# Seven PSUM banks in place of five for one block of seven matmul groups

## The chip, the cores and the metric

The kernel runs on one core of a Trainium2 chip. Its metric is the time of one execution in device microseconds. Matmuls run on TensorE (PE in the profile), elementwise work on VectorE (DVE), ScalarE (ACT) and GpSimd (POOL); SyncE (SP) issues the transfers of weights. A core has eight PSUM banks of 128 x 512 fp32 values in this program, named b0 to b7.

## The reference

One layer of a hybrid decoder for 1024 prompt tokens and 64 sample tokens of width 1024, in fp32. The part that matters here is its MLP:

```python
h2 = rmsnorm(x, lw['g_mlp'])
x = x + jnp.square(jax.nn.relu(h2 @ lw['w_up'])) @ lw['w_down']     # w_up 1024 x 4096, w_down 4096 x 1024
```

Ahead of it stand the input projection, an RWKV-7 mixer, a short convolution and a stick-breaking attention; behind it a gate on a per-layer embedding.

## The kernel before

The tokens are split into two groups. Group A is 512 tokens, group B the other 576 (512 prompt tokens and the 64 of the sample), in two chunks of 288. The 4096 columns of the MLP are taken in 16 blocks of 256. For each block an `up` step computes 256 rows of relu squared (transposed: hidden rows on the partitions), and a `down` step multiplies them with 256 rows of `w_down` and adds the result to the residual `x`. Every fp32 operand is split into a high part in fp32r and a low part, the rest; a product is three matmuls (high by high, low by high, high by low), which are the lines L1094 to L1096 of the ordinary product (`gemm_p`) and L1453 to L1455 of the one below.

Group B's `up` step is `up7`. It computes its 2 x 2 blocks (two halves of the 256 columns by two halves of the 576 tokens) from seven products instead of eight, in the manner of Strassen and Winograd. `block_sums` (L1437 to L1440) forms four sums of weight blocks on DVE from two raw tiles `wr`; `split_piece` (L1074, L1075) casts each of the seven weight pieces to its high part `wh` or `wsh` on ACT and subtracts it for the low part `wl` or `wsl` on POOL or DVE. `seven` then issues the products in a fixed order of the source: (2,2), (3,3), (1,1), (11,11), (12,21), (4,22), (22,4), the first number being the weight piece and the second the operand, each 12 matmuls into one PSUM bank. ACT copies (11,11) out of PSUM as `p1` (L1461). DVE adds (L1509): `u2` = (2,2) + p1, `u3` = (3,3) + u2, `v` = (1,1) + u2, and the four results, each formed in the PSUM bank of the product that comes last for it. `out` (L1500 to L1502) takes a result from its bank with relu and the norm's factor (DVE), squares it (ACT), casts it to `ah` (ACT) and subtracts for `al` (POOL). `down` (L1522) has 16 products of 6 matmuls per block, each added to `x` by DVE.

The raw tiles `wr` have two buffers. A block uses them four times, two for `w_up` and two for `w_down`, each 512 KB, so that a transfer starts when DVE, ACT and POOL are done with what the buffer held before. Pieces `wh` and `wl` have ten buffers, `wsh` and `wsl` four.

Banks are handed out in turn by a function that `banks` returns:

```python
up_bank, down_bank = banks(0, 1, 2, 3, 4), banks(5, 6, 7)      # L1570
u = up7(B, 0, ops, hpb)
for fb in range(1, 16):
    u, before = up7(B, fb, ops, hpb), u
    down(*before, bank=down_bank)
```

The `up` step of block fb stands ahead of the `down` step of block fb - 1. The sixth product of a block so gets the bank of its first, the seventh that of its second, and the next block goes on from there. The order in which each engine has its instructions is not that of the source: a scheduler (L1748) sets it for the whole program ahead of the run, from its own estimates, so that a change of buffers in one place can move instructions from there to the end. On the chip each engine then takes them strictly in that order, and each waits for what it needs.

Group A's last products, ahead of `up7`, use the banks b0 to b5 in turn, and the norm of group B b6 and b7.

Of the kernel before, what the change touches and what calls it, by code (L numbers as in the profile page):

```python
# [48 lines left out]
def hybrid_step(ctx: ExitStack, tc: tile.TileContext, I, O):  # L49
# [6 lines left out]
    def f(t):  # L56
        return t.bitcast(F32)
# [9 lines left out]
    def banks(*ids):  # L67

        turn = itertools.cycle(ids)

        def take():
            i = next(turn)
            return psum.tile([128, 512], F32, name=f"b{i}", bufs=1)

        return take
# [782 lines left out]
    for hf in range(2):  # L858
        for n in range(3):
            w = W.load(w_in[:, SB0 + 512 * n + 256 * hf:SB0 + 512 * n + 256 * hf + 256])  # L860
# [210 lines left out]
    def split_piece(src, sub=None, pool=None, tag="w", bufs=10):  # L1071
        hl = [(pool or wpool).tile([128, 512], F32R, name=f"{tag}{e}", bufs=bufs) for e in "hl"]
        h3, l3 = (t.rearrange("p (k c) -> p k c", k=src.shape[1]) for t in hl)
        S.copy(h3, src)  # L1074
        (sub or G).tensor_sub(l3, src, f(h3))  # L1075
        return hl
# [354 lines left out]
    def block_sums(src, c0, s_, raw=(None, None)):  # L1431


        r = [raw_weights(src, 4 * k, 4, c0, 256, raw[k]) for k in range(2)]
        a = {(m, k): r[k][:, :, 128 * m:128 * m + 128] for m in range(2) for k in range(2)}
        s_ = [t.rearrange("p (k c) -> p k c", k=4) for t in s_]
        V.tensor_add(s_[0], a[1, 0], a[1, 1])  # L1437
        V.tensor_sub(s_[1], s_[0], a[0, 0])
        V.tensor_sub(s_[2], a[0, 0], a[1, 0])
        V.tensor_sub(s_[3], a[0, 1], s_[1])  # L1440
        return {2: s_[1], 3: s_[2], 1: s_[0], 11: a[0, 0], 12: a[0, 1], 4: s_[3], 22: a[1, 1]}

    def seven(w, ops, n, bank, held, add, out, behind=(), order=None):


        behind = iter(behind)

        def product(i, j):
            o = bank()[:, :n]
            wh, wl = (t.rearrange("p (k c) -> p k c", k=4) for t in w[i])  # L1450
            x = ops[j]
            for k in range(4):
                PE.matmul(o, wh[:, k], x[:, 0, k], start=k == 0, stop=False)  # L1453
                PE.matmul(o, wh[:, k], x[:, 1, k], start=False, stop=False)  # L1454
                PE.matmul(o, wl[:, k], x[:, 0, k], start=False, stop=k == 3)  # L1455
            next(behind, None)
            return o

        def first():
            p1 = held("p1")  # L1460
            S.copy(p1, product(11, 11))  # L1461
            return p1

        if order == "11 first":
            p1 = first()
            u2 = add("u2", product(2, 2), p1)
            u3 = add("u3", product(3, 3), u2)
            q5, q4 = product(1, 1), None
        else:
            q6, q7, q5 = product(2, 2), product(3, 3), product(1, 1)  # L1470
            q4 = product(22, 4) if order == "22 early" else None
            p1 = first()
            u2 = add("u2", q6, p1)
            u3 = add("u3", q7, u2)
        v = add("v", q5, u2)
        out(1, 1, add("c", q5, u3))
        if q4 is not None:
            out(1, 0, add("c", q4, u3))
        out(0, 0, add("c", product(12, 21), p1))
        out(0, 1, add("c", product(4, 22), v))  # L1480
        if q4 is None:
            out(1, 0, add("c", product(22, 4), u3))

    def up7(p, fb, ops, pool):


        s_ = [p.act("s", F32) for _ in range(2 * (fb == 0))]
        s_ = [s_[i // 2][:, i % 2, :512] if fb == 0 else pool.tile([128, 512], F32, name=f"s{i}") for i in range(4)]
        ws = {} if fb == 0 else dict(pool=pool, tag="ws", bufs=4)
        t = block_sums(w_up, fb * 256, s_)  # L1490
        w = {i: split_piece(t[i], **ws) if i < 11 else split_piece(t[i]) for i in t}
        n = p.n // 2
        ah, al = p.act("ah", F32R), p.act("al", F32R)
        ends = []

        def out(m, e, c):

            t = slice(e * n, e * n + n)
            r = p.tmp("c")[:, :n]
            V.scalar_tensor_tensor(r, c, 0.0, p.rb[:, t], op0=ALU.max, op1=ALU.mult)  # L1500
            S.square(r, r)
            ends[:] = [S.copy(ah[:, m, t], r), G.tensor_sub(al[:, m, t], r, f(ah[:, m, t]))]  # L1502

        def held(name):
            return pool.tile([128, n], F32, name=name)

        def add(name, c, t):
            r = c if name == "c" else held(name)
            V.tensor_add(r, c, t)  # L1509
            return r  # L1510

        seven(w, ops, n, up_bank, held, add, out)
        last_up[:] = ends
        return p, fb, ah, al

# [46 lines left out]
    ops = B.operands("g_mlp", (2, 3, 1, 4), mpb, 4)  # L1562
# [6 lines left out]
    hpb = tc.alloc_tile_pool(name="h_b", bufs=1, reuse_waits="tile")  # L1569
# [5 lines that stand above are left out]
# [124 lines left out]
    ops = {}  # L1699
    for m, end in enumerate(itertools.chain.from_iterable(gate(A, sl) for sl in range(4))):  # L1700
# [8 lines left out]
        if m == 6:  # L1709
            w = {}  # L1710
# [6 lines left out]
    for sl in range(4):  # L1717
        after = {}
        gate7(B, sl, ops, w, gate7_weights(sl + 1, after) if sl < 3 else ())
        w = after  # L1720
# [31 lines left out]
```

## Time and profile before

| | |
|---|---|
| median of 3 runs | 1705.01 us (1703.33 to 1708.07) |
| the profiled execution | 1706.69 us, of which the span from first to last instruction is 1705.1 |
| PE busy | 1637.8 us, 96% of the span |
| DVE, ACT, POOL busy | 65%, 48%, 43% |
| group B's MLP, from its first product to about its last | 1174.5 to about 1540 us |
| mean granted TensorE clock | 0.987 |

All times of the trace are in us from the start of the span. Matmuls are pipelined, so a row of the timeline shows 0.29 us for a matmul of 288 columns while the next one starts 0.13 us later; whether PE loses time is read from the starts, or from the idle time in brackets that a row shows ahead of it. In a timeline, "x2" is two instructions merged into one row, and a row of SP gives the time from the first issue to the end of the last. In the chain of waits a piece of a transfer gives the time from its issue to its landing.

### The profile page before, as it was taken

What the parts mean: (1) busy time and instruction counts of PE and PEld (TensorE: products, weight loads), DVE (VectorE), ACT (ScalarE), POOL (GpSimd) and SP (SyncE); (2) the same over time, 40 slices, a digit from 0 to 9 for tenths busy, and PEclk for the clock granted to TensorE, in tenths of its full rate; (3) what the DMA queues carried; (4) which work ended last, traced back from release to release, by engine and by line L of the source; (5) the groups of instructions that cost most, each with busy time, mean ns of one, the idle gap of its engine ahead of it and who ended that gap; (6) DMA issues with size and microseconds to landing.
All of it is one profiled execution on the core that took longest, in us unless ns stands there. A gap on an engine that the chain in (4) does not pass through costs nothing.

```text
span 1705.1 us, 30847 instructions
## 1 busy us (share of the span) xinstructions
PE 1637.8 (96%) x11853; PEld 1476.2 (87%) x11853; DVE 1105.0 (65%) x1918; ACT 820.7 (48%) x1627; POOL 727.3 (43%) x778
## 2 busy tenths in 40 slices
PE   6999899999899889999999999999999999999898
PEld 5899888889898767888887778987999999999698
DVE  6266844555277759888854345378777777764986
ACT  6633433343343657666543444364444334436753
POOL 4123121123232664443434654366655445538621
PEclk9999999999999999999999999999999999999999
DMA  5134466325523763433245665322322222323232
GB/s 189 49 120 124 142 166 178 72 78 158 160 66 96 226 170 124 137 121 116 78 121 149 187 178 189 112 84 77 97 90 87 87 87 90 98 76 105 87 120 56
DMA packets 212372, 202.26 MB, mean 119 GB/s; under 512 B 58305, under 2 KB 177761, under 8 KB 212098
## 3 DMA queue, kind: packets, MB, share of 16 engines
q1 hardware_dynamic: 202498, 179.33, 35.4%
q0 software_dynamic: 5120, 16.78, 3.3%
q10 hardware_dynamic: 4608, 4.20, 1.0%
q8 instruction: 93, 1.52, 0.4%
q14 instruction: 53, 0.43, 0.1%
HBM read 163.27 MB, written 36.98 MB: 117 GB/s over the span
## 4 chain that ended last, share of the span: by engine, by line
PE 76%; DVE 10%; DMA 6%; ACT 3%; issue 3%; SPq 2%; POOL 1%; ACTq 0%; DVEq 0%; POOLq 0%
PE b L1094 12%; PE b L1096 11%; PE b L1095 11%; PE b L1453 4%; PE b L1455 4%; PE b L1454 4%; PE b L169 3%; PE b L170 3%; PE b L171 3%; PE b L797 2%; PE b L795 2%; PE b L796 2%; PE b L942 2%; DMA wr<-in_w_in 1%; PE b L512 1%
## 5 line engine op out<-in xcount | busy, mean ns | idle before, releaser
L1075 POOL TENSOR_TENSOR wl<-wr,wh 128x512 fp32r<-128x512 f32 x182 | 255.1, 1411 | 265.5 <-ACT wh L1074 226.3
L1074 ACT CAST wh<-wr 128x512 fp32r<-128x512 f32 x308 | 187.9, 621 | 308.9 <-PE b L1095 198.0
L1522 DVE TENSOR_TENSOR x<-b,x 128x288 f32<-128x288 f32 (+1 forms) x384 | 199.2, 528 | 97.2 <-PE b L1096 86.0
L1094 PE MATMUL b<-ah,wh 128*128 128x288 f32 (+1 forms) x768 | 253.7, 331 | 3.2 <-DVE x L1522 2.1
L1096 PE MATMUL b<-ah,wl 128*128 128x288 f32 (+1 forms) x768 | 252.2, 328 | 0.0
L1095 PE MATMUL b<-al,wh 128*128 128x288 f32 (+1 forms) x768 | 252.0, 328 | 0.0
L1094 PEld LDWEIGHTS b<-ah,wh 128*128 128x128 f32 x768 | 144.5, 188 | 15.3 <-DVE x L1522 4.8
L1096 PEld LDWEIGHTS b<-ah,wl 128*128 128x128 f32 x768 | 144.5, 188 | 10.2
L1095 PEld LDWEIGHTS b<-al,wh 128*128 128x128 f32 x768 | 144.6, 188 | 9.3 <-DVE al L1426 0.3
L1094 PE MATMUL b<-nh,wh 128*128 128x512 f32 x320 | 129.1, 403 | 5.4 <-DVE x L1413 3.3
L795 PE MATMUL b<-wh,h_hi 128*128 128x256 f32 x432 | 127.4, 295 | 5.1 <-ACT sq L805 5.1
L1095 PE MATMUL b<-nl,wh 128*128 128x512 f32 x320 | 128.1, 400 | 0.0
L1096 PE MATMUL b<-nh,wl 128*128 128x512 f32 x320 | 127.7, 400 | 0.0
L797 PE MATMUL b<-wh,h_lo 128*128 128x256 f32 x432 | 126.8, 293 | 0.0
L796 PE MATMUL b<-wl,h_hi 128*128 128x256 f32 x432 | 124.7, 289 | 0.0
L1075 DVE TENSOR_TENSOR wl<-wr,wh 128x512 fp32r<-128x512 f32 x126 | 102.4, 815 | 26.4 <-ACT wh L1074 22.4
L159 POOL TENSOR_TENSOR wl<-wr,wh 128x1024 fp32r<-128x1024 f32 x26 | 64.6, 2500 | 123.0 <-ACT wh L158 118.0
L169 PE MATMUL b<-h_hi,wh 128*128 128x384 f32 (+1 forms) x336 | 115.1, 342 | 1.9 <-ACT xs L333 1.3
L170 PE MATMUL b<-h_lo,wh 128*128 128x384 f32 (+1 forms) x336 | 113.8, 339 | 0.3 <-DVE h_lo L201 0.3
L171 PE MATMUL b<-h_hi,wl 128*128 128x384 f32 (+1 forms) x336 | 112.5, 335 | 0.0
L922 DVE TENSOR_TENSOR_SCAN keep<-keep,onesq 128x128 f32<-128x128 f32 (+3 forms) x64 | 95.3, 1488 | 21.4 <-POOL keep L920 20.7
L1453 PE MATMUL b<-op,wh 128*128 128x288 f32 x320 | 95.0, 297 | 0.1
(437 smaller groups left out, 4450.6 us busy)
## 6 DMA issues: line engine op xcount, KB each, us to landing
wr<-in_w_up SPq DMA_DIRECT2D x64, 512.0 KB
wr<-in_w_down SPq DMA_DIRECT2D x64, 512.0 KB
wr<-in_w_in SPq DMA_DIRECT2D x26, 512.0 KB
wr<-in_w_out SPq DMA_DIRECT2D x16, 512.0 KB
wr<-in_w_ple_gate SPq DMA_DIRECT2D x16, 512.0 KB
xt<-in_x_prompt SPq DMA_DIRECT2D x8, 512.0 KB
stk_s<-sth ACTq DMA_DIRECT2D x32, 128.0 KB
stk_s<-stl SPq DMA_DIRECT2D x32, 128.0 KB
```

The source lines that it names most:

```text
L169: PE.matmul(ps[:, :n], wh[:, k, c], a, start=(k == 0), stop=False)
L170: PE.matmul(ps[:, :n], wh[:, k, c], b, start=False, stop=False)
L171: PE.matmul(ps[:, :n], wl[:, k, c], a, start=False, stop=(k == nk - 1))
L795: PE.matmul(o, a, w[0][:, k, :], start=(k == 0), stop=False)
L797: last = PE.matmul(o, b, w[0][:, k, :], start=False, stop=(k == 7))
L1074: S.copy(h3, src)
L1075: (sub or G).tensor_sub(l3, src, f(h3))
L1094: PE.matmul(ps[:, :n], w(0, k, m), a, start=(k == 0), stop=False)
L1095: PE.matmul(ps[:, :n], w(0, k, m), b, start=False, stop=False)
L1096: PE.matmul(ps[:, :n], w(1, k, m), a, start=False, stop=(k == nk - 1))
L1453: PE.matmul(o, wh[:, k], x[:, 0, k], start=k == 0, stop=False)
L1522: V.tensor_add(p.x[:, m, t0:t0 + n], ps[:, :n], p.x[:, m, t0:t0 + n])
```

## The change

For group B's first block the seven products get banks of their own, b0 to b6, handed out once; the five banks of `up_bank` are first taken up by the second block, which so starts at b0. Nothing else in the source differs (a blank line moves the lines behind by one: L1522 is L1523 there).

```diff
@@ -1509,7 +1509,8 @@
             V.tensor_add(r, c, t)
             return r

-        seven(w, ops, n, up_bank, held, add, out)
+
+        seven(w, ops, n, up_bank if fb else banks(*range(7)), held, add, out)
         last_up[:] = ends
         return p, fb, ah, al
```

The order of the engines' instructions is the same up to the fifth product of the first block and differs from there. Names below are a tile with its buffer number; b3_13057 is the fourth product, (11,11), of block 0, b4_13083 its fifth, b0_13102 or b5_13102 its sixth, b1_13121 or b6_13121 its seventh; 13182, 13195, 13208, 13222, 13248, 13267 and 13286 are block 1's products (2,2), (3,3), (1,1), (11,11), (12,21), (4,22) and (22,4); 13325 is block 0's first `down` product.

PE before, from the last matmul of block 0's fifth product; each row that is shown is the first of a product's 12:

```order
L1455 MATMUL b4_13083<-op21_12763,wl_13004 128x288
L1453 MATMUL b3_13195<-op3_12691,wsh_13156 128x288
...
L1453 MATMUL b0_13102<-op22_12764,wh_13007 128x288
...
L1453 MATMUL b1_13121<-op4_12693,wh_13011 128x288
...
L1453 MATMUL b2_13182<-op2_12690,wsh_13152 128x288
...
L1453 MATMUL b4_13208<-op1_12692,wsh_13160 128x288
...
L1453 MATMUL b0_13222<-op11_12762,wh_13164 128x288
...
L1453 MATMUL b1_13248<-op21_12763,wh_13168 128x288
...
L1094 MATMUL b5_13325<-ah_13015,wh_13307 128x288
```

PE with the change, over the same stretch:

```order
L1455 MATMUL b4_13083<-op21_12763,wl_13004 128x288
L1453 MATMUL b5_13102<-op22_12764,wh_13007 128x288
...
L1453 MATMUL b6_13121<-op4_12693,wh_13011 128x288
...
L1453 MATMUL b0_13182<-op2_12690,wsh_13152 128x288
...
L1453 MATMUL b1_13195<-op3_12691,wsh_13156 128x288
...
L1453 MATMUL b3_13222<-op11_12762,wh_13164 128x288
...
L1453 MATMUL b2_13208<-op1_12692,wsh_13160 128x288
...
L1453 MATMUL b4_13248<-op21_12763,wh_13168 128x288
...
L1094 MATMUL b5_13325<-ah_13015,wh_13307 128x288
```

Block 0's last two products now stand ahead of block 1's first; before, block 1's (3,3) stood ahead of them. Block 1's (11,11) is halved around (1,1).

DVE before, at block 1's additions; wl_13621 and wl_13625 are low parts of block 1's `w_down`, from the raw tile wr_13618:

```order
L1440 TENSOR_TENSOR s3_13456<-wr_13459,s1_13454 128x512
L1509 TENSOR_TENSOR u2_13236<-b2_13182,p1_13221 128x288
L1509 TENSOR_TENSOR u3_13238<-b3_13195,u2_13236 128x288
L1509 TENSOR_TENSOR v_13240<-b4_13208,u2_13236 128x288
L1075 TENSOR_TENSOR wl_13621<-wr_13618,wh_13620 128x512
L1509 TENSOR_TENSOR b1_13248<-b1_13248,p1_13221 128x288
L1509 TENSOR_TENSOR b4_13208<-b4_13208,u3_13238 128x288
L1075 TENSOR_TENSOR wl_13625<-wr_13618,wh_13624 128x512
```

DVE with the change:

```order
L1440 TENSOR_TENSOR s3_13456<-wr_13459,s1_13454 128x512
L1509 TENSOR_TENSOR u2_13236<-b0_13182,p1_13221 128x288
L1509 TENSOR_TENSOR b4_13248<-b4_13248,p1_13221 128x288
L1075 TENSOR_TENSOR wl_13621<-wr_13618,wh_13620 128x512
L1509 TENSOR_TENSOR u3_13238<-b1_13195,u2_13236 128x288
L1509 TENSOR_TENSOR v_13240<-b2_13208,u2_13236 128x288
L1075 TENSOR_TENSOR wl_13625<-wr_13618,wh_13624 128x512
L1509 TENSOR_TENSOR b2_13208<-b2_13208,u3_13238 128x288
```

The addition `u3` of block 1, which reads the bank of (3,3), stood ahead of wl_13621 and now stands behind it.

DVE with the change, from block 0's first additions to `x` on; s2_13768 is a weight sum of block 2 (L1439), wl_13631 a low part of block 1's second half of `w_down`:

```order
L1500 SCALAR_TENSOR_TENSOR c_13300<-b1_13286,rb_12589 128x288
L1439 TENSOR_TENSOR s2_13768<-wr_13770 128x512
L1075 TENSOR_TENSOR wl_13631<-wr_13628,wh_13630 128x512
L1523 TENSOR_TENSOR x_9357<-b6_13333,x_9357 128x288
L1523 TENSOR_TENSOR x_9357<-b5_13325,x_9357 128x288
L1523 TENSOR_TENSOR x_9357<-b7_13341,x_9357 128x288
L1523 TENSOR_TENSOR x_9357<-b5_13349,x_9357 128x288
```

Before, the additions of b6_13333 and b5_13325 stood ahead of s2_13768 and that of b7_13341 right behind it; now all three stand behind it and behind wl_13631.

## The prediction, on record before the run

> **What bounds the kernel now.** First the page: how much of the span TensorE works, and what the chain that ended last is made of.
>
> ```profile
> span 1705.1 us, 30847 instructions
> PE 1637.8 (96%) x11853; PEld 1476.2 (87%) x11853; DVE 1105.0 (65%) x1918; ACT 820.7 (48%) x1627; POOL 727.3 (43%) x778
> PE 76%; DVE 10%; DMA 6%; ACT 3%; issue 3%; SPq 2%; POOL 1%; ACTq 0%; DVEq 0%; POOLq 0%
> ```
>
> PE is the bound, so a change of banks can only give back time in which PE waits. The windows tell where that is: the first block's products up to the fifth, the stretch after them, the rest of the loop, and the gate at the end.
>
> ```profile
> core 0: us, PE busy (x) PEld busy (x) DVE busy (x) ACT busy (x) POOL busy (x), PEclk, DMA share, GB/s
> 1174.50:1182.50 8.00, 8.00 (x61) 7.91 (x59) 4.84 (x5) 2.84 (x6) 5.91 (x5) 1.00 0.30 92
> 1182.50:1210.00 27.50, 23.91 (x175) 23.05 (x174) 22.08 (x39) 15.00 (x33) 19.01 (x17) 1.00 0.35 108
> 1210.00:1540.00 330.00, 330.00 (x2492) 330.00 (x2491) 239.74 (x486) 135.01 (x280) 170.90 (x150) 1.00 0.30 91
> 1540.00:1705.00 165.00, 152.10 (x958) 139.28 (x956) 123.92 (x215) 91.76 (x183) 76.65 (x56) 0.97 0.30 88
> ```
>
> PE loses 27.50 - 23.91 = 3.6 us between 1182.5 and 1210, and nothing at all in the 330 us behind, at full clock. So this one stretch is what the change can touch directly. The waits of PE from 1165 to 1545 are three:
>
> ```profile
> PE b L1453 <- ACT p L1461: 1.5, 1, 1.5
> PE b L1453 <- DVE c L1500: 1.2, 1, 1.2
> PE b L1094 <- DVE x L1522: 0.7, 1, 0.7
> ```
>
> The timeline of PE gives their places (start, duration, and in brackets the idle time):
>
> ```profile
> 1182.37 0.29 PE L1455 MATMUL b<-op,wl 128*128 128x288 f32 x1
> 1184.18 0.40 PE L1453 MATMUL b<-op,wsh 128*128 128x288 f32 x1 [1.52 <-ACT p L1461]
> 1184.42 0.29 PE L1454 MATMUL b<-op,wsh 128*128 128x288 f32 x1
> 1186.17 0.40 PE L1453 MATMUL b<-op,wh 128*128 128x288 f32 x1
> 1190.82 0.40 PE L1453 MATMUL b<-op,wsh 128*128 128x288 f32 x1 [1.20 <-DVE c L1500]
> 1191.20 0.29 PE L1455 MATMUL b<-op,wsl 128*128 128x288 f32 x1
> 1197.19 0.29 PE L1455 MATMUL b<-op,wl 128*128 128x288 f32 x1
> 1208.15 0.40 PE L1094 MATMUL b<-ah,wh 128*128 128x288 f32 x1 [0.74 <-DVE x L1522]
> ```
>
> From 1191.20 to 1197.19 stand 45 steps (the third to the last of 48 matmuls of block 1): 5.99 / 45 = 0.133 us each. That is the price of a matmul below. 1182.37 is the last matmul of block 0's fifth product. By the order of PE, 159 matmuls stand between it and the one at 1208.15 (block 0's last two products and block 1's seven 108, five `down` products 30, 21 of block 2). They need 160 x 0.133 = 21.3 us and took 1208.15 - 1182.37 = 25.8: **4.5 us are lost**, the three waits, a hidden hold of 0.3 at 1186.17, and about 0.1 at each restart (1184.18 to 1184.42 is 0.24 for one step). 4.5 us is 0.26% of the run, less than the 0.3% that a measurement of this kernel can tell from no change. Even a complete success stays within that.
>
> **The change part by part.** No instruction of work is added or removed; the same matmuls, additions, casts and 512 KB transfers stand in another order. So the sum is one of waits, and I walk PE through the new order. The other engines give the times at which a bank comes free; these rows are DVE and ACT before.
>
> ```profile
> 1185.67 0.44 DVE L1509 TENSOR_TENSOR u<-b,p 128x288 f32<-128x288 f32 x1
> 1186.40 0.67 DVE L1075 TENSOR_TENSOR wl<-wr,wh 128x512 fp32r<-128x512 f32 x1
> 1187.00 0.44 DVE L1509 TENSOR_TENSOR u<-b,u 128x288 f32<-128x288 f32 x1
> 1190.31 0.81 DVE L1500 SCALAR_TENSOR_TENSOR c<-b,rb 128x288 f32<-128x288 f32 x2
> 1193.39 1.19 DVE L1438 TENSOR_TENSOR s<-s,wr 128x512 f32<-128x512 f32 x1
> 1196.99 0.46 DVE L1509 TENSOR_TENSOR u<-b,p 128x288 f32<-128x288 f32 x1 [0.71 <-ACT p L1461]
> 1199.53 1.24 DVE L1075 TENSOR_TENSOR wl<-wr,wh 128x512 fp32r<-128x512 f32 x1 [1.22 <-ACT wh L1074]
> 1200.68 0.46 DVE L1509 TENSOR_TENSOR b<-b,p 128x288 f32<-128x288 f32 x1
> 1206.47 1.26 DVE L1439 TENSOR_TENSOR s<-wr 128x512 f32<-128x512 f32 x1 [1.24 <-POOL al L1502]
> ```
>
> ```profile
> 1195.19 0.43 ACT L1502 CAST ah<-c 128x288 fp32r<-128x288 f32 x1
> 1196.57 0.39 ACT L1461 COPY p<-b 128x288 f32<-128x288 f32 x1
> 1198.87 1.14 ACT L1074 CAST wh<-wr 128x512 fp32r<-128x512 f32 x2 [1.92 <-DMA wr<-in_w_down]
> ```
>
> Removed, the 1.52 us. Before, block 1's (3,3) took b3 and waited for the copy `p1` of block 0. Now block 0's sixth and seventh products go to b5 and b6, which nobody holds, with weights split long before: 24 matmuls from 1182.50 to 1185.70.
>
> Kept in part. Block 1's (2,2) now takes b0 and needs block 0's `u2` (1185.67, 0.44), the release for which the sixth product began at 1186.17 before. So PE waits 0.5 us and goes on at 1186.17, 12 matmuls ahead of before. (3,3) in b1 needs `u3` (1187.00, 0.44) at 1187.77: free. Half of (11,11) follows until 1190.2. (1,1) takes b2 and needs the relu (L1500) that ends after 1190.31; DVE gets there no sooner, since the row L1439 ahead of it waits for a transfer. Before, (2,2) waited for the same release and began at 1190.82; so does (1,1), and the 1.20 us shrink to 0.65. Then 30 matmuls to 1194.8 and six of `down` to 1195.6.
>
> Added, small waits. ACT now casts two weight sums (0.57 each, half of the 1.14 of two such casts) ahead of the two `ah` of block 0's last products; the second ends near 1196.0, against 1195.19 + 0.43 = 1195.6. Then block 2's (3,3) takes b3 and waits for `p1` of block 1 (1196.57 + 0.39), and block 1's (4,22) in b0 for `u2` (1196.99 + 0.46). PE loses about 1.2 us here in three pieces, and finishes (4,22) at 1199.1. Two `al` on POOL move behind two more weight pieces; PE needs them after 1202, so that is covered by the matmuls between.
>
> Added, the large wait. Block 1's (22,4) in b1 needs `u3`, which DVE now has behind wl_13621, and that waits for a transfer of `w_down` and its cast. What is queued behind the wait on DVE: `u3`, `v`, wl_13625, the relus of block 1, and all additions to `x`; who waits for these: PE. The transfers in the chain of waits:
>
> ```profile
> 1194.64 4.21 DMA wr<-in_w_down
> 1202.50 3.88 DMA wr<-in_w_up
> ```
>
> The trace does not show this wait; its bounds are these. Late end: the transfer lands as before (1194.64 + 4.21), the low part takes 1.24 from 1199.53, the next addition starts at 1200.68 and ends at 1201.1. Early end: DVE has one addition fewer ahead of L1438 (0.37 from start to start), and I allow another 0.2 for L1438 itself, so the transfer is 0.6 earlier, and the low part takes 0.67: 1200.0. PE resumes between 1200.0 and 1201.1, having lost 0.9 to 2.0 us; I take 1200.5, the middle, since it depends on whether POOL runs beside it. The Trainium skill, "SBUF — State Buffer", section "Who interferes with whom", says that a DVE instruction with two SBUF inputs contends with a GpSimd instruction reading SBUF; 0.67 and 1.24 us agree with it, and by it alone the late end would hold.
>
> 53 matmuls follow, 7.1 us: 1207.1 to 1208.2. Next is a `down` product in b6, which needs the addition of b6_13333, now behind the weight sum L1439 and wl_13631. L1439 waits for a `w_up` transfer, issued when wl_13625 is done: `u3`'s end, `v` 0.37, the low part 0.67 to 1.24, so 1201.0 to 1202.8, landing 3.88 later, 1204.9 to 1206.6. L1439 (0.69 to 1.26), wl_13631 (0.67 to 1.24) and the addition (0.44) follow: 1206.6 to 1209.4. PE goes on at the later of both, 1207.1 to 1209.4, I take 1208.1, with 160 matmuls done. Before it had these at 1208.15 + 0.13 = 1208.3. **The sum is -0.2 us, from -1.2 to +1.1.** What the free banks give is taken back by the wait for the transfer, since the raw tiles come no sooner.
>
> Behind this, blocks 2 to 15 take their banks from the same five in turn as before, so a bank comes back after five products and the demand on DVE is the same: no wait in 330 us, with DVE busy 239.74 of 330, 73%. The order of the gate changes in a few single places. I count nothing for either. The profiled execution of 1706.69 us (span 1705.1) lies 1.7 above the median 1705.01; with -0.2 it would be 1706.5, and the median 1704.8.
>
> **The rivals.**
> All three waits go (gain): the transfer comes early enough that wl_13621 holds nothing. Then up to 4.5 us come back, 1700.5. For it: all three waits are for banks. Against it: the 4.21 us from issue to landing stand in the trace, and DVE's order puts `u3` behind them. The Trainium skill's "Perfetto Trace Analysis", section "Matmul Optimizations", asks that all 8 banks be used for instruction-level parallelism; by that alone it would be this case.
>
> The entry gets worse (small loss): the late ends add up, or the transfer lands later than 4.21 us after its issue: +1.1 to +4 us, 1706 to 1709. For it: two waits of DVE for transfers now stand between PE and its banks. Against: PE has up to 53 matmuls of other work.
>
> The loop stalls (slower): the new order of DVE, with `x` additions behind the weight sums, starves the three `down` banks in every block. DVE's waits for `w_up` in the loop are
>
> ```profile
> L1439 DVE TENSOR_TENSOR s<-wr 128x512 f32<-128x512 f32 x15 | 14.1, 939 | 11.6 <-DMA wr<-in_w_up 10.3 <-POOL al L1502 1.2
> L1437 DVE TENSOR_TENSOR s<-wr 128x512 f32<-128x512 f32 x15 | 11.6, 773 | 11.2 <-DMA wr<-in_w_up 11.2
> ```
>
> 21.5 us in 15 blocks, 1.4 a block. If half of it reached PE in 14 blocks, that is 10 us: 1715. It decides from the point where a bank's addition comes later than its next turn, three `down` products and about 18 matmuls of `up` between, some 36 x 0.133 - 0.8 = 4 us. Against it: these waits are there before, and PE shows none.
>
> **How the numbers follow.** Forecast 0.60, small loss 0.19, gain 0.12, stalling loop 0.09. The predicted time is the forecast's, 1704.8. The range goes from the gain's 1700.5 to the small loss's 1709.0; both also cover the spread of the runs (1703.33 to 1708.07). Faster by over 0.3% (5.1 us) needs the whole gain and luck of the measurement, a third of 0.12, and 0.02 for the gate: 0.06. Slower: the stalling loop and 0.01 of the small loss, 0.10. Same 0.84.
>
> **What would show it.** Right: no wait of PE for `p1` near 1182, one of about 0.5 for `u`, one of about 0.6 for the relu, one of 1 to 2 us for `u` with DVE waiting for `w_down` just before; PE's idle time between 1182.5 and 1210 near 3.5 us again; none from 1210 to 1540. Wrong: no wait behind wl_13621 (gain), or PE idle inside the loop (stall), or a gate whose 12.9 us of idle time (165.00 - 152.10) changes by more than 2.

## The result, and the profile after

The changed kernel takes 1711.27 us (median of 20 runs), the kernel before 1705.32 us in 20 runs on the same chip: a ratio of **1.0029, 95% interval 1.0018 to 1.0040**, about 5 us slower. The forecast was 1704.8 us and no measurable change. The profiled execution of the change takes 1711.43 us with a span of 1709.4.

First the same views as in the prediction. The page of the change (span, busy times, engines' shares of the chain that ended last):

```profile
span 1709.4 us, 30865 instructions
PE 1642.1 (96%) x11853; PEld 1478.0 (86%) x11853; DVE 1112.6 (65%) x1918; ACT 820.4 (48%) x1627; POOL 729.3 (43%) x778
PE 74%; DVE 11%; DMA 6%; ACT 3%; issue 3%; SPq 2%; POOL 1%; DVEq 0%; ACTq 0%; POOLq 0%
```

The page alone says nothing: as many instructions of each engine, the same shares. The windows of the entry, the loop behind it and the gate (busy time and count of each engine, granted clock, DMA share, GB/s):

```profile
1182.50:1210.00 27.50, 24.52 (x172) 22.76 (x170) 20.90 (x35) 14.10 (x32) 21.49 (x18) 1.00 0.39 123
1210.00:1540.00 330.00, 328.13 (x2470) 327.43 (x2471) 244.12 (x485) 130.80 (x272) 166.90 (x146) 1.00 0.29 89
1540.00:1709.40 169.40, 157.87 (x990) 144.76 (x988) 126.85 (x221) 96.13 (x192) 81.46 (x61) 0.97 0.29 89
```

The entry has 27.50 - 24.52 = 3.0 us of idle PE, 3.6 before. The loop, which had none in 330 us, now has 330.00 - 328.13 = 1.9 (part of it belongs to a wait of the entry that ends at 1210.42). Where they lie, by the timeline of PE (start, duration, idle time and what ended it in brackets; lines behind L1511 count one more than before):

```profile
1187.49 0.40 PE L1453 MATMUL b<-op,wsh 128*128 128x288 f32 x1 [0.28 <-DVE u L1509]
1192.17 0.40 PE L1453 MATMUL b<-op,wsh 128*128 128x288 f32 x1 [0.42 <-DVE c L1500]
1197.58 0.87 PE L1094 MATMUL b<-ah,wh 128*128 128x288 f32 x3 [0.36 <-ACT ah L1502]
1198.73 0.40 PE L1453 MATMUL b<-op,wsh 128*128 128x288 f32 x1 [0.28 <-ACT p L1461]
1202.25 0.40 PE L1453 MATMUL b<-op,wh 128*128 128x288 f32 x1 [1.16 <-DVE u L1509]
1210.42 0.41 PE L1094 MATMUL b<-ah,wh 128*128 128x288 f32 x1 [0.89 <-DVE x L1523]
1229.96 0.40 PE L1094 MATMUL b<-ah,wh 128*128 128x288 f32 x1 [0.67 <-DVE x L1523]
1234.81 0.40 PE L1094 MATMUL b<-ah,wh 128*128 128x288 f32 x1 [0.59 <-DVE x L1523]
1246.42 0.40 PE L1453 MATMUL b<-op,wsh 128*128 128x288 f32 x1 [0.20 <-DVE u L1509]
```

The first six are the waits that the prediction named, in its order. The last three it didn't have. All clock times here are 1.35 later than before (block 0 begins at 1175.9 in place of 1174.5; the instructions ahead of it are the same in both kernels, and the other profiles below show starts from 1167.9 to 1180.2, so this is how executions differ). The rows of DVE behind the two long waits and behind the new ones:

```profile
1200.92 0.90 DVE L1075 TENSOR_TENSOR wl<-wr,wh 128x512 fp32r<-128x512 f32 x1 [1.39 <-ACT wh L1074]
1201.75 0.44 DVE L1509 TENSOR_TENSOR u<-b,u 128x288 f32<-128x288 f32 x1
1202.48 1.32 DVE L1075 TENSOR_TENSOR wl<-wr,wh 128x512 fp32r<-128x512 f32 x1
1207.61 1.17 DVE L1439 TENSOR_TENSOR s<-wr 128x512 f32<-128x512 f32 x1 [1.05 <-DMA wr<-in_w_up]
1208.70 1.29 DVE L1075 TENSOR_TENSOR wl<-wr,wh 128x512 fp32r<-128x512 f32 x1
1209.92 1.17 DVE L1523 TENSOR_TENSOR x<-b,x 128x288 f32<-128x288 f32 x3
1218.49 0.69 DVE L1437 TENSOR_TENSOR s<-wr 128x512 f32<-128x512 f32 x1 [1.87 <-DMA wr<-in_w_up]
1229.46 1.17 DVE L1523 TENSOR_TENSOR x<-b,x 128x288 f32<-128x288 f32 x3
1233.58 0.80 DVE L1439 TENSOR_TENSOR s<-wr 128x512 f32<-128x512 f32 x1 [2.95 <-DMA wr<-in_w_up]
1234.31 1.17 DVE L1523 TENSOR_TENSOR x<-b,x 128x288 f32<-128x288 f32 x3
```

The addition `u` stands behind a low part `wl` that waits for a transfer of `w_down` and its cast. The three additions to `x` at 1209.92 stand behind L1439 and a low part. Those at 1229.46 stand behind two low parts of `w_down`, the first of which DVE can start at 1226.89 only, after a transfer and its cast. Those at 1234.31 stand behind L1439, for which DVE is idle for 2.95 us, and PE resumes 0.50 after they start.

One number compares executions with different starts: the **loop interval**, from the start of block 0's first product to the last row L1453 of block 15 that reads a weight sum (`wsh`). It was 1174.5 to 1533.5 = 359.0 us before, and is 1175.9 to 1537.0 = 361.1, which is 2.1 us more. The expectations below are stated in it. It doesn't hold the same work in every kernel, though. In the change, a product of `down` that stood ahead of this row before stands behind it (start and name of three rows of PE with the change):

```profile
1537.00 0.29 PE L1453 MATMUL b<-op,wsh 128*128 128x288 f32 x1
1537.66 0.30 PE L1094 MATMUL b<-ah,wh 128*128 128x288 f32 x1
1539.66 0.29 PE L1455 MATMUL b<-op,wl 128*128 128x288 f32 x1
```

Its six matmuls are 0.8 us by which the interval is too short. The **same-work interval** ends at the last matmul of block 15's products instead (1539.66 here, 1535.36 before), with 2688 matmuls in it in every kernel: 360.8 us before, and 363.8 now. So 3.0 us lie in the loop between these two executions. Behind it stand 169.7 us against 169.8 before. Between span and time lie 1711.43 - 1709.4 = 2.0 us, 1.6 before.

### The profile page after: what moved, and what is told of

It reads as the page before. It is cut to its first block, busy times and chain, and to the rows that moved or that the text cites. A ratio compares the mean times of both kernels' runs of the same rounds, so it can differ in the third digit from the quotient of the medians.

```text
span 1709.4 us, 30865 instructions
## 1 busy us (share of the span) xinstructions
PE 1642.1 (96%) x11853; PEld 1478.0 (86%) x11853; DVE 1112.6 (65%) x1918; ACT 820.4 (48%) x1627; POOL 729.3 (43%) x778
## 3 DMA queue, kind: packets, MB, share of 16 engines
q8 instruction: 93, 1.52, 0.4%
## 4 chain that ended last, share of the span: by engine, by line
PE 74%; DVE 11%; DMA 6%; ACT 3%; issue 3%; SPq 2%; POOL 1%; DVEq 0%; ACTq 0%; POOLq 0%
PE b L1094 11%; PE b L1096 11%; PE b L1095 11%; PE b L1453 4%; PE b L1455 4%; PE b L1454 4%; PE b L169 3%; PE b L170 3%; PE b L171 3%; PE b L797 2%; DMA wr<-in_w_up 2%; PE b L795 2%; PE b L796 2%; PE b L942 2%; DMA wr<-in_w_in 1%
## 5 line engine op out<-in xcount | busy, mean ns | idle before, releaser
L1523 DVE TENSOR_TENSOR x<-b,x 128x288 f32<-128x288 f32 (+1 forms) x384 | 198.2, 527 | 100.2 <-PE b L1096 89.5
L1075 DVE TENSOR_TENSOR wl<-wr,wh 128x512 fp32r<-128x512 f32 x126 | 109.1, 867 | 19.2 <-ACT wh L1074 14.4
L1453 PE MATMUL b<-op,wh 128*128 128x288 f32 x320 | 95.0, 297 | 1.2 <-DVE u L1509 1.2
```

The source lines that it names most:

```text
L1523: V.tensor_add(p.x[:, m, t0:t0 + n], ps[:, :n], p.x[:, m, t0:t0 + n])
```

## The experiments

Theory A: the order of DVE costs the time, additions behind weight sums and low parts that wait for a transfer. Theory B: the 5 us lie elsewhere, in the gate or ahead of the loop. Theory C: the banks themselves, which block 0 now shares with `down`. Ratios are to the kernel before, timed on the same chip.

### The change and the kernel before, again

> The change once more, nothing edited: it gives a second profile of the same order. Theory A (order of DVE): the loss sits where PE waits for additions that stand behind weight sums or low parts which wait for a transfer; so from the first L1453 to the last product of block 15 it takes 361.1 us again (359.0 before), and PE waits again for u (1.2) and x (0.9, 0.7, 0.6) between 1200 and 1235. Theory B (elsewhere): this interval comes out near 359 to 360 and the 5.9 us between the medians of 20 runs lie in the gate or ahead of group B. Time about 1711 by both, ratio to the kernel before 1.003.

> The kernel before against itself, for a second profile and for what the comparison shows where nothing differs: ratio 1.000 with an interval that holds 1, and 1.57 us between span and time. So far there is one profile of the kernel before (359.0 us from the first L1453 to the last product of block 15) and the change's excess by times (about 4 us) is larger than by that interval (1.7 to 2.1). Theory A alone (all of it is in the loop): this profile comes out at 357 to 358. Theory A with a part that the interval doesn't hold: 358.6 to 359.4, with waits 1.5 (p1), 1.2 (relu), 0.7 (x) as before.

> The kernel before, a third profile: the same interval within 0.3 us of the other two and the same three waits. If the interval varies by over 1 us from one execution to the next, one profile can't place an effect of 2 us.

> The change, a third profile and a third ratio (1.0029 and 1.0016 so far): ratio 1.0015 to 1.003, interval 360.4 to 361.4, the waits u 1.2, x 0.9 and two or three x waits of 0.5 to 0.7 in blocks 2 and 3, 2.1 us between span and time (2.08 in both so far). If stretches at half clock behind a stall, as in the runs with the low parts on POOL and with the extra transfer (14 steps of 0.24 us), also come in the change in some executions, a profile shows one here and the interval is 362.5.

> The change, a fourth profile, for the same: interval 360.4 to 361.4, or 362.5 with a stretch at half clock.

| | loop interval, us | same-work interval, us | ratio | time less span, us |
|---|---|---|---|---|
| kernel before | 359.0, 358.1, 358.0 | 360.8, 359.9, 359.9 | 1.0001 (0.9985 to 1.0016) | 1.57 |
| the change | 361.1, 360.7, 361.0, 361.1, 360.6 | 363.8, 363.4, 363.6, 363.8, 363.3 | 1.0029, 1.0016 (1.0002 to 1.0030), 1.0032 (1.0018 to 1.0046), 1.0043 (1.0027 to 1.0058) | 2.08 |

(The fifth profile and fourth ratio are from the last runs below.) The change repeats to 0.5 us, with the same waits in the same places; no profile of it has a stretch at half clock. The kernel before doesn't repeat: the profile that the prediction rests on is the long one. Its third wait (0.74 for `x` at 1208) is missing in the other two. In the third profile of the kernel before, the waits of PE in the whole loop and the window 33 to 67 us behind the start of block 0:

```profile
PE b L1453 <- ACT p L1461: 1.6, 1, 1.6
PE b L1453 <- DVE c L1500: 0.9, 1, 0.9
...
1206.00:1240.00 34.00, 34.00 (x258) 34.00 (x258) 25.04 (x49) 14.37 (x30) 17.80 (x15) 1.00 0.29 93
```

Two waits, and no idle PE where the first profile had one. With means of 360.2 and 363.6 for the same work, the change costs **3.4 us in the loop**. Time less span is the same in every run of a kernel (1.50 to 1.64 before, 2.03 to 2.16 after): another **0.5 us lie outside the span**. The last 8 us of both traces show the same instructions in the same places to 0.2 us, so it isn't the end; what it is stays open.

### Two ordering edges on DVE

```diff
+                    with tc.issue_after(after) if after else nullcontext():   # in load
+                        w.hl[...] = split_piece(r3[:, :, c:c + cp], sub)
-        w = load(w_down[fb * 256:fb * 256 + 256, :], 2, 1024, sub=sub)
+        w = load(..., sub=sub, after=done[("v", 1)] if fb == 1 and p is B else None)
...
+        with tc.issue_after(after) if after else nullcontext():               # L1439, in block_sums
             V.tensor_sub(s_[2], a[0, 0], a[1, 0])
+        t = block_sums(w_up, fb * 256, s_, after=done["x", B, 0, 0, 0] if fb == 3 else None)
```

`done` keeps the instructions of `u`, `v` and `x`; an edge holds the order of issue on one engine and adds no wait for an end.

> Seven banks, with two ordering edges on DVE and nothing else: the first low part of block 1's down weights (wl_13621) stays behind v of block 1, and the weight sum L1439 of block 3 behind block 0's first addition to x (the additions b6_13333 and b5_13325 then stand ahead of it). Theory A: the waits of 1.16 (u), 0.89, 0.67 and 0.59 us (x) go with about 0.1 us of restart each, 3.7 us in all, except that the transfers follow 0.8 us later: the interval from the first L1453 to the last product of block 15 falls from 361.1 to 357.5 to 358.5, the time from 1711.3 to 1707.7 to 1708.7. Theory B: the interval falls by as much, but that much of the time is not lost in it: the time stays above 1709.5. Theory C (the banks themselves: products in b5 and b6, which down uses next, delay the loop whatever DVE's order is): no change, 361 and 1711.

> Seven banks with the first of the two edges alone: wl_13621 behind v of block 1. Only two rows of DVE change places. Theory A: the wait for u at 1202 (1.16 us) goes or falls below 0.3, but wl_13621 and wl_13625 end 0.7 us later, so the transfer of w_up behind them, L1439 and the addition b6_13333 come 0.7 later while PE arrives 1.2 earlier: the wait for x grows from 0.9 to 2 to 3 us, and the interval is 361 again, the time 1710.5 to 1711.5. Theory C: the same 361 and 1711. A rival (the wait for u is what matters): 359.9 and 1710.

> Seven banks with the second of the two edges alone: the weight sum L1439 of block 3 stays behind block 0's first addition to x, so on DVE two additions to x stand ahead of it in place of behind. Theory A (order of DVE): the wait for u at the first L1453 + 26 us stays at 1.2, the waits for x (0.9 at + 34 us, then 1.3 in two to three pieces) fall below 0.3 in all; the interval from the first L1453 to the last product of block 15, 361.1 and 360.7 in the two profiles of the change, becomes 358.7 to 359.5, the ratio to the kernel before 0.999 to 1.001. Theory C (the banks): 361 and 1.002. If the wait for u only passes on what the transfer takes, the x waits come back at another place and the interval stays above 360.

| edges | loop interval | same work | ratio |
|---|---|---|---|
| none (the change) | 360.9 | 363.6 | see above |
| first: low part behind `v` | 359.6 | 362.2 | 1.0010 (0.9995 to 1.0024) |
| second: L1439 behind `x` | 359.0 | 360.9 | 1.0006 (0.9990 to 1.0022) |
| both | 357.9, 357.9, 358.1 | 359.8, 359.8, 359.9 | 0.9997 (0.9986 to 1.0007), 1.0006 (0.9994 to 1.0019) |

PE's waits in the loop with both edges (line, what for, us in total, times, longest):

```profile
PE b L1095 <- ACT ah L1504: 0.3, 1, 0.3
PE b L1455 <- ACT p L1463: 0.3, 1, 0.3
PE b L1455 <- DVE u L1511: 0.3, 1, 0.3
PE b L1455 <- DVE c L1502: 0.2, 1, 0.2
```

The wait for `u` behind the low part is gone, and every wait for `x`. With both edges the seven banks cost nothing: 359.8 against 360.2 for the same work, a ratio of 1.000 in both measurements. Theory A holds, C falls as far as the banks alone go: they are the same here.

The first edge alone refutes a part of A. It was to gain nothing, since the transfer behind the low parts was to come later; it gained 1.3 us. The additions `u` and `v` moved into the time in which DVE waits for the cast, and no longer stood between the two low parts, so these ended 0.85 us earlier (26.9 us behind block 0's start, 27.7 in the change). The second edge gained 2.7 us for the same work and left the wait for `u` at 1.2, as expected; its order has the `down` product back ahead of the interval's last row, so the loop interval shows 1.9.

### Other numbers of banks, other banks

> Six banks for block 0 (b0 to b5), so only its sixth product gets a bank of its own; the seventh takes b0 again and waits for u2, block 1 begins at b0. In DVE's order one addition to x (b6_13333) stays ahead of the third weight sum, where the change has none and the kernel before has two. Theory A: between the two, interval 359.5 to 360.5, time 1707.5 to 1709.5. Theory C (banks): half the loss, the same numbers, but with the waits at the banks b5 and b6 of down and not behind the weight sums. Theory B: interval as it may, the time within 2 us of the change's 1711.

> Seven banks again, but b0 to b4, b6 and b7: the last two products go to b6 and b7, so that down's first bank b5 is free from the start. The order of every engine is that of the change, row for row; only the banks differ. Theory A: the same waits (u 1.2, x 0.9 and the two or three behind), interval 360.4 to 361.4, ratio 1.0015 to 1.003. Theory C (sharing b5 and b6 with down is what costs): the x waits go or fall by half, interval 358.5 to 359.7, ratio within 0.999 to 1.001.

```diff
-        seven(w, ops, n, up_bank if fb else banks(*range(7)), held, add, out)
+        seven(w, ops, n, up_bank if fb else banks(*range(6)), held, add, out)
...
+        seven(w, ops, n, up_bank if fb else banks(0, 1, 2, 3, 4, 6, 7), held, add, out)
```

Six banks: interval 358.7 (same work 360.6), ratio 1.0013 (0.9999 to 1.0027), no wait for `x`, but two for `u` (1.8), one for `al` (0.9), one for the relu (0.6). The interval came out below the expected 359.5 to 360.5; by the same work five, six and seven banks take 360.2, 360.6 and 363.6, so there is no even scale between them.

With b6 and b7 every engine has the rows of the change in the change's order. The interval was 359.5 (same work 362.1), and 1.0029 (1.0016 to 1.0042) the ratio. PE had the six waits of the entry, the 1.2 for `u` and the 0.9 for `x` among them, but the two for `x` in blocks 2 and 3 were gone:

```profile
PE b L1453 <- DVE u L1509: 1.8, 3, 1.2
PE b L1094 <- DVE x L1522: 0.9, 1, 0.9
```

The reason stands in a transfer. In the change the `w_up` transfer behind block 1's low parts is issued at 1213.40 and takes 4.99 us by the chain of waits; with b6 and b7 it is issued at 1210.04 and the sum that needs it starts 3.88 later. The first fence is the change, the second the other kernel: half microseconds from 3.0 or 3.5 us behind the issue on (last two columns: DMA share, GB/s), then the DMA queues' packets, MB and share in the 3.0 us from the issue on:

```profile
1213.40 4.99 DMA wr<-in_w_up
...
1216.40:1216.90 0.50, 0.50 (x6) 0.50 (x5) 0.22 (x1) 0.00 (x0) 0.49 (x1) 1.00 0.33 113
1216.90:1217.40 0.50, 0.50 (x6) 0.50 (x5) 0.00 (x0) 0.00 (x0) 0.00 (x0) 1.00 0.06 8
1217.40:1217.90 0.50, 0.50 (x6) 0.50 (x5) 0.00 (x0) 0.00 (x0) 0.00 (x0) 1.00 0.07 14
...
q1 hardware_dynamic: 449, 0.46, 54.1%
q8 instruction: 1, 0.02, 2.0%
```

```profile
1210.04 0.37 SPq L1068 DMA_DIRECT2D wr<-in_w_up  x1
1213.92 0.69 DVE L1437 TENSOR_TENSOR s<-wr 128x512 f32<-128x512 f32 x1 [0.66 <-DMA wr<-in_w_up]
...
1213.54:1214.04 0.50, 0.50 (x6) 0.50 (x5) 0.12 (x1) 0.14 (x1) 0.00 (x0) 1.00 0.00 0
...
q1 hardware_dynamic: 477, 0.49, 57.1%
```

In the change the last few KB (8 and 14 GB/s over 1 us, the share of one engine in 16) come 1 us later. Something else is on the DMA engines there: one 16 KB packet of an instruction queue, which takes about 1 us. In the change it starts 2.6 us behind the issue, while the transfer is under way, and the transfer's last packet ends at 4.5; with b6 and b7 it starts at 3.27, when the transfer's last packet ends. Two more profiles, and a third with the runs below, were to tell chance from cause:

> Seven banks with b6 and b7 in place of b5 and b6, a second profile. Theory A (order of DVE and the transfer): it shows the x waits of blocks 2 and 3 (0.6 to 0.7 each) whenever the w_up transfer behind block 1's low parts takes 5 us and not when it takes 3.9; with 5 us the interval is 361.0 to 361.4. Theory C (banks): the x waits are gone whatever the transfer takes, 359.7.

> The same kernel, a third profile: theory A 361.0 to 361.4 with a transfer of 5 us or 359.7 with one of 3.9; theory C 359.7 in any case.

> Both edges, a second profile: interval 358.0 to 358.5 (358.2 before), no wait for x or for u over 0.4 behind the first block, also if the w_up transfer takes 5 us, since two additions to x stand ahead of the sum that waits for it.

The interval was 359.1, 359.0 and 359.0 (the third of these with the runs below; same work 361.8, 361.7, 361.7), with no `x` wait in blocks 2 and 3. From issue to the start of the sum L1437 it is 3.7 to 3.9 us in the four profiles of this kernel, and 4.9 to 5.3 in the five of the change. So it isn't chance: the straggler belongs to one kernel and not to the other, though their rows are the same. Nor is it the banks by themselves: with b5 and b6 and the first edge it is there too (5.1 us), with b5 and b6 and the second edge or both it isn't (3.8 to 3.9). What goes with it is the instruction packet. In these six profiles it starts 2.1 to 3.0 us behind the issue, and the transfer's last packet ends at 4.3 to 4.8. In 13 others it starts at 3.0 to 3.3, and the last packet ends at 3.3 to 3.4; the extra transfer below is the one exception, with 3.1 and 4.2. By its result this is what theory C said, by its mechanism what A said: the waits of blocks 2 and 3, 363.6 - 361.8 = 1.8 us, come when that transfer is late **and** DVE has `x` behind the sums. Why the packet comes later against the transfer with other banks, no run shows. In the kernels with the second edge the transfer takes 3.8 to 3.9 us, so they don't tell how much of the 1.8 the order alone would have saved.

### Less and more to wait for

```diff
-        down(*before, bank=down_bank)
+        down(*before, bank=down_bank, sub=G if fb == 2 else V)    # low parts of block 1's down weights on POOL
```

> Seven banks, and the low parts of block 1's down weights (wl_13621, wl_13625, wl_13631 and the fourth) are made on POOL in place of DVE, so that nothing on DVE waits for that w_down transfer; the additions to x then stand ahead of the weight sums in the order. Theory A: the wait for u and those for x go, interval 357.8 to 359, ratio 0.9985 to 1.0005. Against it: POOL makes the al of the same blocks, which come later by up to four low parts; if that decides, PE waits for al 1 to 3 us and the interval is 359.5 to 361.

```diff
         r = [raw_weights(src, 4 * k, 4, c0, 256, raw[k]) for k in range(2)]
+        if c0 == 768:
+            SP.dma_start(r[0], src[0:512, c0:c0 + 256].rearrange("(k p) c -> p k c", p=128))
```

> Seven banks, and the first 512 KB of block 3's up weights are fetched twice into the same tile, so that the weight sum L1439 of block 3 may start some 4 us later; the planner answers with three additions to x ahead of that sum, where the change has none. Theory A: with more to move the loop gets shorter: the wait for u stays (1.2), the waits for x fall below 0.5 in all, interval 358.7 to 359.7, ratio 0.999 to 1.001. Theory D (the transfers bound the first blocks whatever the order of DVE is): everything behind the second transfer comes 3.7 us later, interval 363 to 365, ratio 1.003 to 1.005.

Neither came out as theory A had it. With the low parts on POOL the interval is 361.1 (same work 363.0, ratio 1.0019, 1.0004 to 1.0035): the long wait for `u` is gone and 0.2 of the first one is left, but one wait for `x` of 2.4 us stands in its place. With the extra transfer it is 362.4 (same work 364.3, 1.0020, 1.0006 to 1.0034; the edit also doubles one transfer of the gate, outside the interval): `u` 1.2 as expected, and `x` 1.9 in two pieces where under 0.5 was expected. The transfer after the doubled one took 5.19 us, so theory D (the transfers set the pace) is nearer for this kernel. Two things made the wait for `x` so long with the low parts on POOL. The transfer that the sum L1439 waits for stands behind two low parts on POOL (2.55 us in the chain of waits) and is issued 30.5 us behind block 0's start, 27.7 to 28.0 in the change. And the sum itself is slow, by the rows of DVE and POOL:

```profile
1205.14 3.61 DVE L1439 TENSOR_TENSOR s<-wr 128x512 f32<-128x512 f32 x1 [5.17 <-DMA wr<-in_w_up]
...
1204.15 1.30 POOL L1075 TENSOR_TENSOR wl<-wr,wh 128x512 fp32r<-128x512 f32 x1
1205.40 1.57 POOL L1502 TENSOR_TENSOR al<-c,ah 128x288 fp32r<-128x288 f32 x2
1206.94 1.26 POOL L1075 TENSOR_TENSOR wl<-wr,wh 128x512 fp32r<-128x512 f32 x1
```

The sum takes 3.61 us where it takes 0.69 alone. POOL works without a gap until 1208.20, so only 3.61 - 3.06 = 0.55 us of it lie beside an idle POOL: this sum made next to no progress while POOL ran. That agrees with the Trainium skill, "SBUF — State Buffer", section "Who interferes with whom", by which DVE's second port is GpSimd's and is held exclusively. It isn't so each time: in the kernel before, 21 DVE instructions of this shape in the loop lie beside a busy POOL for practically their whole length, and they took 0.68 to 1.60 us. Why this one was held so much longer, no run shows.

And behind the wait PE is slow. The window with the wait, the one behind it, and the next, with the granted clock in the third column from the right:

```profile
1206.60:1210.00 3.40, 1.03 (x8) 0.84 (x7) 3.24 (x4) 0.00 (x0) 1.60 (x2) 1.00 0.15 27
1210.00:1213.40 3.40, 3.40 (x16) 3.40 (x15) 1.10 (x3) 0.62 (x1) 1.17 (x1) 0.50 0.40 132
1213.40:1216.80 3.40, 3.40 (x28) 3.40 (x27) 2.87 (x6) 0.92 (x2) 1.70 (x2) 1.00 0.00 0
```

14 matmuls start 0.240 us apart in place of 0.133: 14 x 0.107 = 1.5 us more. The same with the extra transfer, behind waits of 1.39 and 0.55 us:

```profile
1216.40:1219.80 3.40, 1.49 (x10) 1.09 (x8) 2.96 (x5) 1.28 (x3) 1.29 (x1) 1.00 0.00 0
1219.80:1223.30 3.50, 3.48 (x14) 3.48 (x15) 3.46 (x9) 1.81 (x4) 3.10 (x3) 0.51 0.46 150
```

### All three on one chip

> Seven banks with b6 and b7, timed once more. If the interval (+0.7) and the time outside the span (+0.5) are all: ratio 1.0007, so 1.000 to 1.0015, and 1.0029 was chance. If something else in that order of the engines costs as much as in the change: 1.002 to 1.0035. Interval 359.3 to 359.7 and a second w_up transfer of 3.9 us in either case.

> The change beside it: ratio 1.0015 to 1.0035 (1.0029, 1.0016 and 1.0032 so far), interval 361.0 to 361.4, second w_up transfer 5.0 us. By interval and time outside the span alone 1.0018.

> Both edges beside it: ratio 0.9990 to 1.0008 (0.9997 so far), interval 358.2, by interval and time outside the span (1.77 against 1.57) alone 0.9999.

Ratios 1.0021 (1.0006 to 1.0036), 1.0043 (1.0027 to 1.0058) and 1.0006 (0.9994 to 1.0019), intervals 359.0, 360.6 and 358.1. Where the loop loses its time shows when two kernels' starts are compared with the same number of matmuls ahead, counted from block 0's first (us behind the mean of the three profiles of the kernel before; less than 0 is ahead of it):

| matmuls ahead | 120 | 160 | 180 | 320 | 400 | 500 | 2687 |
|---|---|---|---|---|---|---|---|
| the change, mean of 5 | -2.4 | -0.8 | +0.6 | +1.3 | +3.0 | +3.5 | +3.4 |
| b6 and b7, mean of 4 | -2.5 | -0.9 | +0.5 | +1.2 | +1.3 | +1.7 | +1.6 |
| both edges, mean of 3 | -2.5 | -0.9 | -0.9 | -0.5 | -0.2 | -0.2 | -0.4 |

The free banks put PE 2.4 us ahead. In the change the small waits for `ah` and `p1` take 1.6 of that back, the long wait for `u` 1.4, the one for `x` behind it and what follows 0.7, and blocks 2 and 3 another 2.2. Behind the 500th matmul nothing is lost.

The four ratios of the change, weighted by their intervals, give 1.0029 (1.0023 to 1.0036), 3.9 to 6.1 us; loop and time outside the span are 3.4 + 0.5 = 3.9. So **0 to 2 us of the change's loss have no place in the profiles**, and it may be none. With b6 and b7 the two ratios give 1.0026 (1.0016 to 1.0036), 2.7 to 6.1 us, against 1.6 + 0.5 = 2.1: there 0.6 to 4 us have no place. The gate isn't it: behind the same-work interval stand 168.2 to 169.7 us in the change, 168.2 to 169.6 with b6 and b7, 168.2 to 169.8 before. For what stands ahead of the loop theory B can't be ruled out, since it differs by up to 12 us between executions, though its instructions are the same. With both edges nothing is left over (-0.4 + 0.2 against a ratio of 1.000).

## Why the prediction was wrong

**What bounds the kernel: right, on a profile that was not the usual one.** PE bounds it, and the entry is where the banks act. But the third of the three waits, 0.74 for `x`, is in one of three profiles of the kernel before. The base of the sum, 4.5 us lost, was 0.9 too long.

**Removed, the 1.52 us: right.** The wait for `p1` at that place is gone in all profiles of the change.

**Kept in part: right, smaller.** 0.28 in place of 0.5 for `u`, 0.42 in place of 0.65 for the relu (0.2 in the other profiles of the change).

**Added, small waits: right in two of three, and larger.** `ah` and `p1` are there with 0.36 and 0.28, that for `u2` is not. The three matmuls at 1197.58 take 0.87 in place of 0.40. The seven steps from 1196.92 to 1199.46 take 2.54 us where 0.133 each would be 0.93, so the piece costs 1.6 in place of 1.2. The large wait takes that up, since its end is set by DVE.

**Added, the large wait: right.** PE resumed at 1202.25; less the 1.35 of the later start this is 1200.90, in the forecast's 1200.0 to 1201.1, and the wait was 1.16 (0.9 to 2.0). The next one, for the addition behind L1439 and a low part, ended at 1210.42 - 1.35 = 1209.07 (1207.1 to 1209.4). From block 0's start to this matmul it is 34.5 us, and before, by the 160 steps of the prediction, 1208.3 - 1174.5 = 33.8: +0.7, in the forecast's -1.2 to +1.1. Against the other two profiles of the kernel before, without the third wait, it would be outside.

**Behind this: the step that failed.** "[A] bank comes back after five products and the demand on DVE is the same: no wait in 330 us ... I count nothing for either." The demand is the same, but not the order. The entry leaves additions to `x` waiting behind weight sums, and DVE takes them up over the next two blocks. There a `w_up` transfer that takes 5.1 us from issue to use, 3.8 before, finds them still behind: 0.67 + 0.59 + 0.20 us of waits and what each costs around it, 2.2 us by the matmul counts in place of none. With b6 and b7, where the transfer isn't late and the two waits for `x` don't come, the loop is 1.8 us shorter.

**The sum against one execution: the second step that failed.** It took over what lies between span and time from the kernel before, 1706.69 - 1705.1 = 1.6 us. It is 2.1 in the change, the same in every run, and no trace of the kernel before could show it.

**The rivals.** The loop did stall, by the mechanism that the third rival named, but in two blocks and for 2.2 us, not in 14 for 10. The point that it gave, an addition later than its bank's next turn, is what the rows at 1229.46 and 1234.31 show. Each case was priced alone. What came is the small loss and a short piece of the stall together, the 0.5 us outside the span, and 0 to 2 us that nothing accounts for. The range ended at 1709.0 because the two were not added.

**What would show it.** PE's idle time at the entry was to be near 3.5 and is 3.0 by the window, 3.4 by the six waits whole; the gate's was 12.9 and is 169.40 - 157.87 = 11.5, within the 2 us; "none from 1210 to 1540" is where the trace said no: 1.9, of which 1.5 are the three waits in blocks 2 and 3.

## What to carry to other kernels

Free banks let the matmuls run ahead, and the scheduler answers with another order on the engine that empties the banks: an addition that frees a bank must not stand behind an instruction that waits for a transfer. Two ordering edges undid the loss, in kernels in which the late transfer was on time too; the same banks with them were worth 0.4 us in the loop, nothing that times can tell, so no version here beats the kernel before. Before a wait is priced from one profile, see whether a second one has it, and follow a changed order at least until the work that it put off is done.

## What the runs showed of the hardware that was not expected

- **A stall of PE costs more than itself.** After a wait of 2.37 us, or of 1.39 and 0.55 close together, with PE busy for 1.03 and 1.49 of 3.4 us, the granted clock was 0.50 for the next 3.4 us and cost 1.5 us. After the single waits of up to 1.56 us in the other kernels the steps were 0.13 us again behind the first. The Trainium skill, "TensorE: Matmul & The Clock Gate", section "Part 1: The HAM clock gate", gives a half clock after a window of about 3.4 us that was idle; length and clock agree, but here a window with PE busy for 30 to 44% of it was enough.
- **A sum on DVE took 3.61 us in place of 0.69** while POOL ran for 3.06 of them without a gap; others of its shape took 0.68 to 1.60 beside a busy POOL in the kernel before.
- **A late tail of a transfer goes with an instruction packet**: one 16 KB packet of an instruction queue takes about 1 us. Where it started 2.1 to 3.0 us behind the issue of a 512 KB transfer (six profiles), the transfer's last packet ended at 4.3 to 4.8 us; where it started at 3.0 to 3.3 (13 profiles), at 3.3 to 3.4. One profile has 3.1 and 4.2. That the packet holds the tail up is the plain reading; no run moved one packet alone.
- **Time outside the span** is a property of the kernel: 1.57 before, 1.71 to 1.77 with six banks, the second edge, both edges, the low parts on POOL or the extra transfer, 2.08 to 2.10 in the others. Each run lies within 0.1 us of its kernel's mean.
